# Fused state-space tables on VectorE, with the skip diagonal and the B clearing on ScalarE

## The chip, the core and the metric

The kernel runs on one core of a Trainium2 chip. The metric is the device time of one execution in microseconds. Three runs of the kernel before gave 884.39, 884.48 and 885.38 us, so the median is 884.48 us.

## The reference, cut to what matters

The program is a decoder trunk of two residual layers and a final RMSNorm, over 256 tokens of width 2048, in float32. Layer 0 projects the normalised input to 5120 columns (xa, ga, u, v, gb). The columns xa go through a complex-diagonal state-space mixer of 64 groups with 64 states each; u, v and gb go through a gated MLP. Layer 1 is differential attention. The change touches the constants of the state-space mixer and one small exponential of layer 1.

```python
dt = exp(log_dt)[:, None]
mag = exp(lr * dt)
ab_re = mag * cos(li * dt)
ab_im = mag * sin(li * dt)
...
bb_re = f_re[..., None] * br - f_im[..., None] * bi
...
# h: scan of the states with a = ab over the 256 positions
y = einsum(h_re, c_re) - einsum(h_im, c_im) + d_skip * u
```

## The kernel before

All weights stream once from HBM in chunks of 1 MB, in the order v, xa, u, gb, ga, then the output projection of layer 0 and the weights of the GLU, then layer 1. A chunk lands in one of three buffers `wr`. It is split into two halves, and each half into two parts so that TensorE can multiply float32 as products of a shorter format: ScalarE writes the rounded part `wh` (line 82, called from `split`, line 193), and VectorE writes the remainder `wl` (line 61, called from line 194). `wh` and `wl` have three buffers each, one per half, so the half number n can be written only when TensorE has finished with the half n - 3. The activations are split the same way into `hh` (ScalarE) and `hl` (VectorE), tile by tile, while the first four chunks are split (`h_split`, line 311). For each weight tile and each token half TensorE runs three matmuls, `wh` with `hh`, `wl` with `hh`, and `wh` with `hl`.

The accumulators of the projections (`main_t`, `main_c`) are tiles of the tag "m" with two buffers. v has two of them (v0, v1), and xa0, the first tile of xa, reuses the buffer of v0. So xa0 can start only when v0 has been read out. That is done by two Gelu activations into `vt` (lines 673 and 674), which need the row scale `rs0` of the RMSNorm of the input; a table load for Gelu stands ahead of them.

The state-space constants are made in the meantime. `ssm_params` (line 388) computes dt and mag with `exact_exp` (line 359), a polynomial exponential of some 20 VectorE operations of 128x32, then the phase with a sine and a cosine polynomial, and seven repeated squarings `pw` (line 461). `e_tables` (line 558) builds for each half a table `E` of the powers of the phase for 128 positions, by doubling: for k = 1 to 6 it multiplies the first 2^k columns by `pw[k]` in blocks of 8 pairs. `ssm_consts` (line 492) clears the tiles `bbr` on GpSimd and fills them later. `diag_skip` (line 481) builds 16 diagonal blocks `intra` from the identity and the skip weights `dq`, on GpSimd.

Nothing of the order is written by hand, except on SyncE's queue. A list scheduler with its own cost model decides in which order each engine's instructions stand; the splits, the Gelu of v and the norm are marked as urgent (`hp()`), the constants are not. Each engine then runs its list strictly in order, so an instruction that waits holds up all that stands behind it.

Of the kernel before, what the change touches and what calls it, by code (L numbers as in the profile page):

```python
# [10 lines left out]
F32 = mybir.dt.float32  # L11
F32R = mybir.dt.float32r
I32 = mybir.dt.int32
AF = mybir.ActivationFunctionType
ALU = mybir.AluOpType
# [14 lines left out]
def hybrid_trunk_kernel(ctx: ExitStack, tc: tile.TileContext, xT, xtok, w_in0, w_glu, w_out0,  # L30
# [20 lines left out]
    def t4(name, shape, dt=F32):  # L51
        return tmp.tile(shape, dt, name=name, tag="t4", bufs=3)
# [10 lines left out]
    def mul(o, a, b):  # L63
        tt(o, a, b, ALU.mult)

    def add(o, a, b):
        tt(o, a, b, ALU.add)
# [4 lines left out]
    def ts(o, a, s1, op0, s2=None, op1=None):  # L72
        if op1 is None:
            V.tensor_scalar(out=o, in0=a, scalar1=s1, scalar2=None, op0=op0)
        else:
            V.tensor_scalar(out=o, in0=a, scalar1=s1, scalar2=s2, op0=op0, op1=op1)
# [278 lines left out]
    def tr32(name, shape=(128, 32), dt=F32):  # L355
        return sm.tile(list(shape), dt, name=name, tag=f"tr{shape[1]}{'i' if dt == I32 else ''}",
                       bufs=(7 if dt == F32 else 1) if shape[1] <= 32 else 2)

    def exact_exp(o, x, w=32):
        sh = (128, w)  # L360
        xc = tr32("e_x", sh)
        ts(xc, x, -104.0, ALU.max, 90.0, ALU.min)
        n = tr32("e_n", sh)
        ts(n, xc, 1.4426950408889634, ALU.mult)
        ts(n, n, MAGIC, ALU.add)
        ts(n, n, MAGIC, ALU.subtract)
        r = tr32("e_r", sh)
        stt(r, n, -0.693359375, xc, ALU.mult, ALU.add)
        stt(r, n, 2.12194440054690583e-4, r, ALU.mult, ALU.add)
        p = tr32("e_p", sh)  # L370
        ts(p, r, 1.0 / 5040, ALU.mult)
        for c in (1.0 / 720, 1.0 / 120, 1.0 / 24, 1.0 / 6, 0.5, 1.0):
            stt(p, p, c, r, ALU.add, ALU.mult)
        ts(p, p, 1.0, ALU.add)
        n1 = tr32("e_n1", sh)
        ts(n1, n, 0.5, ALU.mult)
        ts(n1, n1, MAGIC, ALU.add)
        ts(n1, n1, MAGIC, ALU.subtract)
        sub(n, n, n1)
        for part in (n1, n):  # L380
            e = tr32("e_i", sh, I32)
            ts(e, part, 127.0, ALU.add, 8388608.0, ALU.mult)
            mul(p, p, e.bitcast(F32))
        V.tensor_copy(out=o, in_=p)

    cst = {}

    def ssm_params():
        dt_ = p32("dt")
        exact_exp(dt_, log_dt)  # L390
        yield
        mag = p32("mag")
        z = tr32("lrdt")
        mul(z, lam_re, dt_)
        exact_exp(mag, z)
        r2 = p32("r2")
        mul(r2, mag, mag)
        cst["r2"] = r2
        yield
        ph = tr32("ph")  # L400
        mul(ph, lam_im, dt_)
        k = tr32("ph_k")
        ts(k, ph, 1.0 / (2 * math.pi), ALU.mult)
        ts(k, k, MAGIC, ALU.add)
        ts(k, k, MAGIC, ALU.subtract)
        stt(ph, k, -6.28125, ph, ALU.mult, ALU.add)
        stt(ph, k, -1.93500518798828125e-3, ph, ALU.mult, ALU.add)
        stt(ph, k, -(2 * math.pi - 6.28125 - 1.93500518798828125e-3), ph, ALU.mult, ALU.add)
        y = tr32("ph_y")
        ts(y, ph, 0.5, ALU.mult)  # L410
        z = tr32("ph_z")
        mul(z, y, y)
        s = tr32("ph_s")
        f = math.factorial
        ts(s, z, 1.0 / f(13), ALU.mult)
        for c in (-1.0 / f(11), 1.0 / f(9), -1.0 / f(7), 1.0 / f(5), -1.0 / f(3)):
            stt(s, s, c, z, ALU.add, ALU.mult)
        stt(s, s, 1.0, y, ALU.add, ALU.mult)
        c_ = tr32("ph_c")
        ts(c_, z, -1.0 / f(14), ALU.mult)  # L420
        for c in (1.0 / f(12), -1.0 / f(10), 1.0 / f(8), -1.0 / f(6), 1.0 / f(4), -0.5):
            stt(c_, c_, c, z, ALU.add, ALU.mult)
        ts(c_, c_, 1.0, ALU.add)
        ep = p32("ep", 64).rearrange("p (c m) -> p c m", c=2)
        mul(ep[:, 0, :], s, s)
        ts(ep[:, 0, :], ep[:, 0, :], -2.0, ALU.mult, 1.0, ALU.add)
        stt(ep[:, 1, :], s, 2.0, c_, ALU.mult, ALU.mult)
        yield
        ab = p32("ab", 64).rearrange("p (c m) -> p c m", c=2)
        mul(ab, ep, mag.unsqueeze(1).to_broadcast([128, 2, 32]))  # L430
        den = tr32("den")
        t1 = tr32("t1")
        mul(den, lam_re, lam_re)
        mul(t1, lam_im, lam_im)
        add(den, den, t1)
        V.reciprocal(out=den, in_=den)
        nr = tr32("nr")
        ts(nr, ab[:, 0, :], 1.0, ALU.subtract)
        fc = p32("fc", 64).rearrange("p (c m) -> p c m", c=2)
        t2_ = tr32("t2")  # L440
        mul(t1, nr, lam_re)
        mul(t2_, ab[:, 1, :], lam_im)
        add(t1, t1, t2_)
        mul(fc[:, 0, :], t1, den)
        mul(t1, ab[:, 1, :], lam_re)
        mul(t2_, nr, lam_im)
        sub(t1, t1, t2_)
        mul(fc[:, 1, :], t1, den)
        fa = p32("fa", 64).rearrange("p (c m) -> p c m", c=2)
        mul(t1, fc[:, 0, :], ab[:, 0, :])  # L450
        mul(t2_, fc[:, 1, :], ab[:, 1, :])
        sub(fa[:, 0, :], t1, t2_)
        mul(t1, fc[:, 0, :], ab[:, 1, :])
        mul(t2_, fc[:, 1, :], ab[:, 0, :])
        add(fa[:, 1, :], t1, t2_)
        cst.update(ab=ab, fc=fc, fa=fa, ep=ep)
        yield

        pw = []
        prev = ep  # L460
        for j in range(7):
            sq = tr32("pw_sq", (128, 64)).rearrange("p (c m) -> p c m", c=2)
            m = tr32("pw_m")
            mul(sq, prev, prev)
            add(m, sq[:, 0, :], sq[:, 1, :])
            ts(m, m, -1.0, ALU.mult, 2.0, ALU.add)
            e = p32(f"pw{j}", 64).rearrange("p (c m) -> p c m", c=2)
            sub(e[:, 0, :], sq[:, 0, :], sq[:, 1, :])
            stt(e[:, 1, :], prev[:, 0, :], 2.0, prev[:, 1, :], ALU.mult, ALU.mult)
            mul(e, e, m.unsqueeze(1).to_broadcast([128, 2, 32]))  # L470
            pw.append(e)
            prev = e
        cst["pw"] = pw
        yield
# [3 lines left out]
    def sc16(ap):  # L478
        return ap.unsqueeze(2).to_broadcast([128, 32, 16])

    def diag_skip():
        intra = t8(11, "intra", [128, 16, 128])
        for i in range(16):
            G.tensor_scalar(out=intra[:, i, :], in0=ident, scalar1=dq[:, i:i + 1], scalar2=None, op0=ALU.mult)
        cst["intra"] = intra

    def masked(dst, src):
# [4 lines left out]
    def ssm_consts():  # L492
        for c in range(2):
            bbr[c] = t8(7 + c, f"bbr{c}", [128, 32, 2, 32])
            G.memset(bbr[c], 0.0)
        cA = t8(9, "cA", [128, 2, 32, 32])
        cN = t8(10, "cN", [128, 2, 32, 32])
        G.memset(cA, 0.0)
# [59 lines left out]
    def e_tables(half):  # L558
        E = big.tile([128, 2, 16, 128], F32, name=f"E{half}", tag="e")
        etab[half] = E  # L560
        hs = slice(half * 16, half * 16 + 16)
        pw = cst["pw"]
        V.memset(E[:, 0, :, 0:1], 1.0)
        V.memset(E[:, 1, :, 0:1], 0.0)
        V.tensor_copy(out=E[:, :, :, 1:2], in_=pw[0][:, :, hs].unsqueeze(3))
        for k in range(1, 7):
            n = 1 << k
            for q in range(2):
                ph = slice(q * 8, q * 8 + 8)
                es = E[:, :, ph, 0:n]  # L570
                sh = [128, 8, n]
                m = [t4(f"em{half}{k}{q}{i}", [128, 2, 8, 64])[:, :, :, 0:n] for i in range(2)]
                for i in range(2):
                    a = pw[k][:, i, half * 16 + q * 8:half * 16 + q * 8 + 8].unsqueeze(2).to_broadcast(sh)
                    for c in range(2):
                        mul(m[i][:, c], es[:, c], a)
                o = slice(n, 2 * n)
                sub(E[:, 0, ph, o], m[0][:, 0], m[1][:, 1])
                add(E[:, 1, ph, o], m[0][:, 1], m[1][:, 0])
            if k >= 4:  # L580
                yield
        yield
# [81 lines left out]
    for n in range(2):  # L664
        ps = main_t(f"v{n}")
        for k in range(4):
            gemm_t(ps, h_acts, range(k * 4, k * 4 + 4), k == 0, k == 3)
            if n == 0 and k == 2:
                diag_skip()
            run_side(2)  # L670
        with hp():
            for t in range(2):
                act(vt[:, t, n * 512:(n + 1) * 512], ps[:, t, :], AF.Gelu_apprx_tanh,
                    scale=rsx[0][:, t:t + 1], accum_out=vsum[:, t, n:n + 1])
# [488 lines left out]
```

## Time and profile before

| | |
|---|---|
| median of three runs | 884.48 us |
| the profiled execution, its own time | 885.88 us |
| its span | 884.2 us |
| TensorE matmul, busy | 867.1 us (98%) |
| VectorE, busy | 678.4 us (77%), 1248 instructions |
| ScalarE, busy | 457.5 us (52%), 637 instructions |
| GpSimd, busy | 36.5 us (4%), 54 instructions |
| TensorE clock granted over the span | 0.998 |

The profile is of one execution. A busy share is an average over stages that have different limits. Matmuls overlap their neighbours, so a matmul's own duration is longer than the step from one to the next, and the step is what counts for the pace. 1.7 us of the profiled execution's time lie outside its span.

### The profile page before, as it was taken

The numbers are of one execution on the slowest core, as the hardware profiler recorded it, in microseconds if no ns is written. First come the engines' busy times: TensorE is split into PE (matmuls) and PEld (weight loads), VectorE is DVE, ScalarE is ACT, GpSimd is POOL, SyncE is SP. The second block draws the span as 40 slices with busy tenths as digits, with TensorE's granted clock in tenths as the row PEclk, the third lists the DMA queues.
The fourth block names the chain that finished last, engine by engine and source line by source line (L and its number), as shares of the span: only waits on it lengthen the run. The fifth ranks groups of instructions, "written<-read, shape, count | busy, mean of one in ns | idle before, by whom it ended". The sixth has DMA issues, their size and how long they took to land.

```text
span 884.2 us, 13006 instructions
## 1 busy us (share of the span) xinstructions
PE 867.1 (98%) x5038; PEld 748.3 (85%) x5038; DVE 678.4 (77%) x1248; ACT 457.5 (52%) x637; POOL 36.5 (4%) x54
## 2 busy tenths in 40 slices
PE   9999999999999999999999999999999999999996
PEld 7799978788999789888788888888888888888885
DVE  8999869999988766577876688667867687665773
ACT  6664862455434655565445544455546544564551
POOL 7100000000000100000000000000000000000001
PEclk9999999999999999999999999999999999999999
DMA  8965452235524655555554555445554555555442
GB/s 289 406 236 193 144 191 95 97 103 184 191 99 145 254 178 184 190 191 171 169 203 153 181 191 191 184 153 184 183 192 154 190 182 189 189 194 199 157 178 95
DMA packets 55166, 160.18 MB, mean 181 GB/s; under 512 B 3392, under 2 KB 37440, under 8 KB 41024
## 3 DMA queue, kind: packets, MB, share of 16 engines
q1 hardware_dynamic: 54240, 155.68, 50.1%
q0 software_dynamic: 576, 3.15, 0.9%
q8 instruction: 39, 0.64, 0.3%
q10 hardware_dynamic: 288, 0.52, 0.2%
q14 instruction: 23, 0.19, 0.1%
HBM read 157.24 MB, written 2.10 MB: 180 GB/s over the span
## 4 chain that ended last, share of the span: by engine, by line
PE 87%; DVE 8%; ACT 2%; issue 1%; DMA 1%; DVEq 0%; ACTq 0%
PE k L251 7%; PE q L251 7%; PE v L225 4%; PE v L226 4%; PE v L224 4%; PE k L252 3%; PE q L252 3%; PE g L226 3%; PE g L225 3%; PE g L224 3%; PE od L225 2%; PE od L224 2%; PE od L226 2%; DVE wl L61 2%; PE ga L237 2%; PE ga L240 2%
## 5 line engine op out<-in xcount | busy, mean ns | idle before, releaser
L82 ACT ACTIVATE wh<-wr 128x1024 fp32r<-128x1024 f32 (+1 forms) x276 | 288.7, 1047 | 339.2 <-PE v L226 59.5
L61 DVE TENSOR_TENSOR wl<-wr,wh 128x1024 fp32r<-128x1024 f32 (+1 forms) x276 | 332.3, 1206 | 135.3 <-ACT wh L82 133.8
L251 PE MATMUL k<-h2p,wh 128*128 128x512 f32 x256 | 90.9, 398 | 1.7 <-DVE rm L61 1.7
L251 PE MATMUL q<-h2p,wh 128*128 128x512 f32 x256 | 90.2, 396 | 0.0
L252 PE MATMUL q<-h2p,wl 128*128 128x256 f32 x256 | 71.9, 284 | 0.2 <-DVE wl L61 0.2
L252 PE MATMUL k<-h2p,wl 128*128 128x256 f32 x256 | 72.0, 282 | 0.0
L251 PEld LDWEIGHTS k<-h2p,wh 128*128 128x128 f32 x256 | 48.1, 188 | 13.3 <-DVE rm L61 2.0
L251 PEld LDWEIGHTS q<-h2p,wh 128*128 128x128 f32 x256 | 47.8, 188 | 10.5
L225 PE MATMUL v<-wl,h2p 128*128 128x512 f32 x128 | 50.8, 397 | 0.0
L225 PE MATMUL g<-wl,h2p 128*128 128x512 f32 x128 | 50.3, 393 | 0.0
L226 PE MATMUL g<-wh,h2p 128*128 128x512 f32 x128 | 50.1, 391 | 0.0
L226 PE MATMUL v<-wh,h2p 128*128 128x512 f32 x128 | 50.0, 391 | 0.0
L224 PE MATMUL g<-wh,h2p 128*128 128x512 f32 x128 | 50.0, 390 | 0.0
L224 PE MATMUL v<-wh,h2p 128*128 128x512 f32 x128 | 50.0, 390 | 0.0
L252 PEld LDWEIGHTS q<-h2p,wl 128*128 128x128 f32 x256 | 48.4, 189 | 1.0 <-DVE wl L61 0.6
L252 PEld LDWEIGHTS k<-h2p,wl 128*128 128x128 f32 x256 | 48.4, 189 | 0.1
L225 PE MATMUL od<-wl,oh 128*128 128x512 f32 x96 | 37.6, 392 | 0.0
L224 PE MATMUL od<-wh,oh 128*128 128x512 f32 x96 | 37.5, 391 | 0.0
L226 PE MATMUL od<-wh,ol 128*128 128x512 f32 x96 | 37.3, 390 | 0.0
L237 PE MATMUL ga<-hh,wh 128*128 128x256 f32 x128 | 36.6, 286 | 0.0
L240 PE MATMUL ga<-hh,wl 128*128 128x256 f32 x128 | 36.5, 287 | 0.0
L239 PE MATMUL ga<-hl,wh 128*128 128x256 f32 x128 | 36.5, 285 | 0.0
(330 smaller groups left out, 2041.1 us busy)
## 6 DMA issues: line engine op xcount, KB each, us to landing
wr<-in_w_in_dram SPq DMA_DIRECT2D x68, 1024.0 KB, 4.8
wr<-in_w_in_dram SPq DMA_DIRECT2D x68, 512.0 KB, 5.2
wr<-in_w_out_dram SPq DMA_DIRECT2D x32, 1024.0 KB, 4.8
wr<-in_w_glu_dram SPq DMA_DIRECT2D x4, 1024.0 KB, 4.7
wr<-in_w_in_dram SPq DMA_DIRECT2D x8, 256.0 KB, 4.9
xk<-in_xtok_dram SPq DMA_DIRECT2D x2, 1024.0 KB, 10.8
xr<-in_xtok_dram POOLq DMA_DIRECT2D x2, 1024.0 KB, 7.2
xt<-in_xT_dram SPq DMA_DIRECT2D x8, 128.0 KB, 4.6
```

What stands on the lines that cost most here:

```text
L61: (eng or V).tensor_tensor(out=o, in0=a, in1=b, op=op)
L82: A.activation(out=o, in_=i, func=f, **kw)
L224: PE.matmul(ps[:, t, :], hi[:, s], wh, start=first and a == 0, stop=False)
L225: PE.matmul(ps[:, t, :], hi[:, s], wl, start=False, stop=False)
L226: PE.matmul(ps[:, t, :], lo[:, s], wh, start=False, stop=last and a == len(ktiles) - 1)
L237: PE.matmul(ps[:, c, :], wh[:, s], hi, start=first and a == 0 and c % 2 == 0, stop=False, skip_group_check=True)
L239: PE.matmul(ps[:, c, :], wh[:, s], lo, start=False, stop=False, skip_group_check=True)
L240: PE.matmul(ps[:, c, :], wl[:, s], hi, start=False, stop=fin, skip_group_check=True)
L251: PE.matmul(ps[:, c, :], wh[:, s], hl, start=first and a == 0, stop=False, skip_group_check=True)
L252: PE.matmul(ps[:, c, T:], wl[:, s], hl[:, 0], start=False, stop=a == len(ktiles) - 1 and not first, skip_group_check=True)
```

## The change

The exponential loses four VectorE operations each time: two scalings are fused with the addition behind them, the final addition of 1 goes into the first product, and the second product writes the result directly. The phase loses one operation, and each of the seven squarings loses one. The power tables multiply both parts (real and imaginary) in one operation, in blocks of up to 16 pairs: a half took 72 operations, and now takes 28. The clearing of `bbr` and the 16 diagonal blocks go from GpSimd to ScalarE, and the call of `diag_skip` stands three chunks later in the program.

```diff
@@ exact_exp
-        ts(n, xc, 1.4426950408889634, ALU.mult)
-        ts(n, n, MAGIC, ALU.add)
+        ts(n, xc, 1.4426950408889634, ALU.mult, MAGIC, ALU.add)
         ts(n, n, MAGIC, ALU.subtract)
...
-        ts(p, p, 1.0, ALU.add)
         n1 = tr32("e_n1", sh)
-        ts(n1, n, 0.5, ALU.mult)
-        ts(n1, n1, MAGIC, ALU.add)
+        ts(n1, n, 0.5, ALU.mult, MAGIC, ALU.add)
         ts(n1, n1, MAGIC, ALU.subtract)
         sub(n, n, n1)
-        for part in (n1, n):
-            e = tr32("e_i", sh, I32)
-            ts(e, part, 127.0, ALU.add, 8388608.0, ALU.mult)
-            mul(p, p, e.bitcast(F32))
-        V.tensor_copy(out=o, in_=p)
+        e = tr32("e_i", sh, I32)
+        ts(e, n1, 127.0, ALU.add, 8388608.0, ALU.mult)
+        stt(p, p, 1.0, e.bitcast(F32), ALU.add, ALU.mult)
+        e = tr32("e_i", sh, I32)
+        ts(e, n, 127.0, ALU.add, 8388608.0, ALU.mult)
+        mul(o, p, e.bitcast(F32))
@@ ssm_params
-        ts(k, ph, 1.0 / (2 * math.pi), ALU.mult)
-        ts(k, k, MAGIC, ALU.add)
+        ts(k, ph, 1.0 / (2 * math.pi), ALU.mult, MAGIC, ALU.add)
...
-            add(m, sq[:, 0, :], sq[:, 1, :])
-            ts(m, m, -1.0, ALU.mult, 2.0, ALU.add)
+            stt(m, sq[:, 0, :], -1.0, sq[:, 1, :], ALU.mult, ALU.subtract)
...
-            mul(e, e, m.unsqueeze(1).to_broadcast([128, 2, 32]))
+            stt(e, m.unsqueeze(1).to_broadcast([128, 2, 32]), 2.0, e, ALU.add, ALU.mult)
@@ diag_skip, ssm_consts
+    def zeros(z):
+        act(z.rearrange("p m j h -> p (m j h)").rearrange("p (a b) -> p a b", b=128),
+            ones.unsqueeze(1).to_broadcast([128, 16, 128]), AF.Copy, scale=0.0)
...
-            G.tensor_scalar(out=intra[:, i, :], in0=ident, scalar1=dq[:, i:i + 1], scalar2=None, op0=ALU.mult)
+            act(intra[:, i, :], ident, AF.Copy, scale=dq[:, i:i + 1])
...
-            G.memset(bbr[c], 0.0)
+            zeros(bbr[c])
@@ e_tables
-            for q in range(2):
-                ph = slice(q * 8, q * 8 + 8)
+            w = min(16, 512 // n)
+            for ph in (slice(z, z + w) for z in range(0, 16, w)):
...
-                    for c in range(2):
-                        mul(m[i][:, c], es[:, c], a)
+                    mul(m[i], es, a.unsqueeze(1).unsqueeze(3).to_broadcast([128, 2, w, n]))
@@ the loop over v
-            if n == 0 and k == 2:
+            if n == 1 and k == 0:
                 diag_skip()
```

The scheduler makes new lists from this. Three places of them follow, before and after; equal rows that stand together are counted (x2).

The first place is the head of ScalarE's list. `warm` is a one-column activation, `hh` a tile of the input's rounded part, and `wr_89` the first chunk. Before:

```order
L82 ACT_TABLE_LOAD
L82 ACTIVATE warm<-ones 128x1
L82 ACTIVATE hh_152<-xt,pkt 128x256
L82 ACTIVATE wh_0_156<-wr_89 128x512
L82 ACTIVATE hh_152<-xt,pkt 128x256
L82 ACTIVATE wh_0_156<-wr_89 128x512
```

And now:

```order
L82 ACT_TABLE_LOAD
L82 ACTIVATE warm<-ones 128x1
L82 ACTIVATE bbr_557<-ones 128x2048
L82 ACTIVATE bbr_559<-ones 128x2048
L82 ACTIVATE intra<-ident,pkt 128x128 x11
L82 ACTIVATE hh_152<-xt,pkt 128x256 x3
L82 ACTIVATE wh_0_156<-wr_89 128x512 x2
```

Both clearings, 11 of the 16 diagonal blocks and two further tiles of `hh` now stand ahead of the first `wh`.

The second place is VectorE's list about the first `wl`, in the projection of v. Before, seven instructions stand ahead of the first `hl`, and the first `wl` comes four small operations behind it:

```order
L79 SCALAR_TENSOR_TENSOR hl_154<-xt,pkt,hh_152 128x256
L79 SCALAR_TENSOR_TENSOR e_r<-e_n,e_r 128x32
L74 TENSOR_SCALAR e_p<-e_r 128x32
L74 TENSOR_SCALAR e_n_231<-e_n 128x32
L79 SCALAR_TENSOR_TENSOR e_p<-e_p,e_r 128x32
L61 TENSOR_TENSOR wl_0_157<-wr_89,wh_0_156 128x512
```

And now:

```order
L79 SCALAR_TENSOR_TENSOR hl_154<-xt,pkt,hh_152 128x256
L79 SCALAR_TENSOR_TENSOR ph<-ph_k,ph 128x32
L79 SCALAR_TENSOR_TENSOR e_p<-e_p,e_r 128x32
L79 SCALAR_TENSOR_TENSOR hl_154<-xt,pkt,hh_152 128x256
L79 SCALAR_TENSOR_TENSOR ph<-ph_k,ph 128x32
L79 SCALAR_TENSOR_TENSOR hl_154<-xt,pkt,hh_152 128x256
L79 SCALAR_TENSOR_TENSOR e_p<-e_p,e_r 128x32
L61 TENSOR_TENSOR wl_0_157<-wr_89,wh_0_156 128x512
```

Ahead of the first `hl` now stand 34 small operations of the two exponentials and the phase, and three `hl` stand ahead of the first `wl`.

The third place is ScalarE's list where v0 is read out. The name wh7_1 is the second half of chunk 7, the last chunk of v; chunk 8 is the first of xa. Before:

```order
L82 ACTIVATE wh7_0_860<-wr7_125 128x1024
L82 ACTIVATE wh7_1_864<-wr7_125 128x1024
L82 ACTIVATE cN_649<-bct_85 64x32x16 x4
L82 ACT_TABLE_LOAD
L82 ACTIVATE vt_210,vsum_211<-v0_402,rs0_186 128x512 x2
L82 ACTIVATE wh8_0_894<-wr8_128 128x1024
L82 ACTIVATE wh8_1_898<-wr8_128 128x1024
```

And now:

```order
L82 ACTIVATE wh7_1_794<-wr7_125 128x1024
L82 ACTIVATE wh8_0_824<-wr8_128 128x1024
L82 ACTIVATE wh8_1_828<-wr8_128 128x1024
L82 ACTIVATE wh9_0_961<-wr9_788 128x1024
L82 ACT_TABLE_LOAD
L82 ACTIVATE vt_210,vsum_211<-v0_386,rs0_186 128x512 x2
L82 ACTIVATE vt_210,vsum_211<-v1_639,rs0_186 128x512 x2
```

The table load and the read-out of v0 moved behind wh8_0, wh8_1 and wh9_0. The buffer of wh9_0 is that of wh7_1, three halves earlier.

## Rows read from the trace of the kernel before

**Rows 1.** The page: the chain that ended last, share of the span by engine.

```profile
PE 87%; DVE 8%; ACT 2%; issue 1%; DMA 1%; DVEq 0%; ACTq 0%
```

**Rows 2.** Busy time in stretches (start:end, length, then busy us by engine, clock, DMA).

```profile
5.50:54.20 48.70, 46.80 (x198) 37.59 (x197) 46.78 (x203) 34.21 (x50) 17.45 (x19) 1.00 0.95 362
54.20:103.70 49.50, 49.50 (x520) 49.11 (x520) 48.49 (x99) 27.00 (x36) 0.00 (x0) 1.00 0.48 171
103.70:288.90 185.20, 181.80 (x1227) 157.55 (x1226) 163.74 (x287) 87.12 (x105) 0.00 (x0) 1.00 0.40 140
```

**Rows 3.** Timeline of ScalarE, start of the program (start us, us, instruction, [idle before]).

```profile
2.10 0.20 ACT L82 ACTIVATE warm<-ones 128x1 f32<-128x1 f32 x1
3.58 0.51 ACT L82 ACTIVATE hh<-xt,pkt 128x256 fp32r<-128x256 f32 x1 [1.27 <-DMA xt<-in_xT_dram]
5.01 0.63 ACT L82 ACTIVATE wh<-wr 128x512 fp32r<-128x512 f32 x1 [0.92 <-DMA wr<-in_w_in_dram]
...
16.25 0.91 ACT L82 ACTIVATE hh<-xt,pkt 128x256 fp32r<-128x256 f32 x2
```

**Rows 4.** Timeline of TensorE, from the warm-up matmuls into v.

```profile
1.13 4.64 PE L298 MATMUL psw<-ones 128*128 128x128 f32 x20 [1.13 <-DVE ones L293]
5.69 0.79 PE L224 MATMUL v<-wh,hh 128*128 128x512 f32 x1
7.47 0.79 PE L225 MATMUL v<-wl,hh 128*128 128x512 f32 x1 [0.99 <-DVE wl L61]
8.06 0.63 PE L226 MATMUL v<-wh,hl 128*128 128x512 f32 x1
8.49 0.63 PE L224 MATMUL v<-wh,hh 128*128 128x512 f32 x1
...
10.58 0.40 PE L226 MATMUL v<-wh,hl 128*128 128x512 f32 x1
10.81 0.39 PE L224 MATMUL v<-wh,hh 128*128 128x512 f32 x1
```

**Rows 5.** Timelines of GpSimd and VectorE: clearings, and what VectorE ran then.

```profile
0.99 3.54 POOL L495 MEMSET bbr<- 128x2048 f32 x2
...
2.73 1.84 DVE L76 TENSOR_SCALAR e_x<-pkt 128x32 f32<-128x32 f32 x1 [1.65 <-DMA pkt<-in_pk_dram]
...
37.06 0.18 DVE L61 TENSOR_TENSOR pw_m<-pw_sq 128x32 f32<-128x32 f32 x1
...
37.23 1.81 POOL L499 MEMSET cN<- 128x2048 f32 x1 [1.03 <-ACT xsq L82]
...
37.36 1.22 DVE L61 TENSOR_TENSOR wl<-wr,wh 128x1024 fp32r<-128x1024 f32 x1
```

**Rows 6.** Timeline of VectorE in the second half's power table, and two plain splits.

```profile
218.55 2.49 DVE L61 TENSOR_TENSOR em<-E,pw 128x512 f32<-128x512 f32 x4
...
223.90 2.39 DVE L61 TENSOR_TENSOR wl<-wr,wh 128x1024 fp32r<-128x1024 f32 x2
```

**Rows 7.** Timeline of ScalarE at the read-out of v0.

```profile
49.12 1.28 ACT L82 ACT_TABLE_LOAD   x1
50.41 0.69 ACT L82 ACTIVATE vt<-v,rs 128x512 f32<-128x512 f32 x1
...
51.09 0.68 ACT L82 ACTIVATE vt<-v,rs 128x512 f32<-128x512 f32 x1
...
51.75 2.00 ACT L82 ACTIVATE wh<-wr 128x1024 fp32r<-128x1024 f32 x2
```

**Rows 8.** Timeline of TensorE, the last matmul of v and the first of xa.

```profile
53.94 0.48 PE L226 MATMUL v<-wh,hl 128*128 128x512 f32 x1
54.25 0.28 PE L237 MATMUL xa<-hh,wh 128*128 128x256 f32 x1
```

**Rows 9.** Timeline of TensorE: a wait within v, and the longest wait after the start.

```profile
43.02 0.50 PE L225 MATMUL v<-wl,hh 128*128 128x512 f32 x1 [0.86 <-DVE wl L61]
...
430.82 0.51 PE L251 MATMUL k<-h2p,wh 128*128 128x512 f32 x1 [1.72 <-DVE rm L61]
```

More of the change, by code (lines that the diff above doesn't have):

```diff
@@ L567, in e_tables @@
             n = 1 << k
-            for q in range(2):
-                ph = slice(q * 8, q * 8 + 8)
+            w = min(16, 512 // n)
+            for ph in (slice(z, z + w) for z in range(0, 16, w)):
                 es = E[:, :, ph, 0:n]
-                sh = [128, 8, n]
-                m = [t4(f"em{half}{k}{q}{i}", [128, 2, 8, 64])[:, :, :, 0:n] for i in range(2)]
+                m = [t4(f"em{half}{k}{ph.start}{i}", [128, 2, w, n]) for i in range(2)]
                 for i in range(2):
-                    a = pw[k][:, i, half * 16 + q * 8:half * 16 + q * 8 + 8].unsqueeze(2).to_broadcast(sh)
-                    for c in range(2):
-                        mul(m[i][:, c], es[:, c], a)
+                    a = pw[k][:, i, half * 16 + ph.start:half * 16 + ph.stop]
+                    mul(m[i], es, a.unsqueeze(1).unsqueeze(3).to_broadcast([128, 2, w, n]))
                 o = slice(n, 2 * n)
```

## The prediction

> **What bounds the kernel now.** I read the page first: the chain that ended last is 87% TensorE [rows 1], and TensorE is busy 98% of the span. So VectorE's saved operations are worth only what TensorE waits for, and a new wait of TensorE is paid in full. Next come the busy times by stretch [rows 2]. From 5.5 to 54.2 us (v) TensorE is idle 48.70 - 46.80 = 1.9 us, from 54.2 to 103.7 (xa) not at all, and from 103.7 to 288.9 (where the power tables are used) 185.20 - 181.80 = 3.4 us. VectorE is busy 46.78, 48.49 and 163.74 us there: near its limit in the first two, and yet TensorE lost nothing in the second. Then the timelines, at three places. At the start the first `wh` runs at 5.01 us for 0.63 [rows 3], and TensorE begins v at 5.69 and goes on at 7.47, after the first `wl` [rows 4]. At the end of v, ScalarE has read out v0 by 51.8 [rows 7], and xa follows v after 0.31 us (53.94 to 54.25) [rows 8]. Last, two waits of TensorE: 0.86 us on a `wl` within v, and 1.72 us at 430.82, the longest after the start [rows 9].
>
> **The change, part by part.** The profiled execution took 885.88 us, 1.7 beyond its span of 884.2, and lies 1.4 above the median; I sum changes of the span and add them to the median.
>
> *The start.* ScalarE now runs two clearings, 11 diagonal blocks and three `hh` ahead of the first `wh`. Two `wh` of 1024 columns take 2.00 us [rows 7], so 2048 columns in one instruction cost about 1.9. For a block: two `hh` of 256 columns take 0.91 [rows 3], some 0.42 from one to the next; the columns cost 2.00/2048 x 128 = 0.12 per 128, which leaves 0.31 for 128. From the warm-up's end at 2.2: 2 x 1.9 + 11 x 0.31 + 3 x 0.42 = 8.5, so the first `wh` starts at 10.7, ends at 11.3, and its `wl` (half of 1.22 [rows 5], and a little) is there at 12.0. TensorE goes on at 12.0 instead of 7.47: **+4.5 us**. If a block costs only what the one-column `warm` does (0.20 [rows 3]) it is 11 x 0.11 = 1.2 less, and if it costs as much as an `hh`, 1.2 more: +3.3 to +5.7. I take the middle because the columns' price is measured on the same engine.
>
> VectorE doesn't set this. Its chain starts with `pkt` at 2.73; 34 operations at 0.18 [rows 5] end at 8.8, before the third `hh`. A fused operation has no row of its own; at up to twice 0.18 the chain would end near 12 and shift the start by about 1 more, which the upper end nearly holds. The first `e_x`, 1.84 us while GpSimd cleared `bbr`, falls to the usual 0.18 [rows 5]: 1.7 us on VectorE, hidden behind ScalarE.
>
> [...]
>
> *GpSimd.* Its 3.54 us of clearings and the blocks behind them go [rows 5]. What follows in its queue is the clearing of `cA`, which waits for the norm anyway, so the empty queue is worth nothing by itself. The trace shows no harm of a GpSimd clearing to a large two-input operation: `wl` took 1.22 us at 37.36, wholly beside `cN` [rows 5], as two of them took 2.39 elsewhere [rows 6]. So I count no faster `hl` or `wl` for the blocks removed. [...]
>
> *SyncE's queue.* The load of the fourth chunk waits for a buffer that the first chunk's splits free, so it slips with the start. TensorE needs it later by as much: 0.
>
> *Within v.* VectorE has about 20 small operations less over the whole program, 0.1 to 0.18 each, thus 2 to 3.6 us, most of them ahead of the tables; and TensorE, coming later, leaves VectorE more time. I let the 0.86 us wait [rows 9] and a little more go: **-1.0** (0 to -1.9, all the idle time of this stretch [rows 2]).
>
> *The read-out of v0.* This is the new wait. `wh9_0` now stands ahead of the table load on ScalarE. Its buffer is that of `wh7_1`, which TensorE reads to the last matmul of v. Only after that come `wh9_0` (0.97), the table load (1.28), and two `vt` (0.69 and 0.68) [rows 7], and only then is the buffer free that xa0 needs. Counted from the start of v's last matmul, which lasts about 0.39 [rows 4]: 0.39 + 0.97 + 1.28 + 0.69 + 0.68 = 4.0, where xa now follows after 0.31 [rows 8]: **+3.7 us**. It is 2.7 if the buffer were free early. It is 4.4 if `rs0`, which the read-out needs too, comes later by four of VectorE's small operations (4 x 0.18). Behind the table load stand v1's read-out and the next `wh`, which xa needs later.
>
> *The tables.* A half takes 28 operations instead of 72, 88 fewer in all. Four of 512 columns took 2.49 us, two of 1024 take 2.39 [rows 6]: 0.05 per operation saved, and more for small ones (a 128x32 one is 0.18, nearly all of it fixed). At 0.06 it is 5.3 us. In the xa stretch TensorE was never idle, so that share is worth nothing; from 103.7 on 3.4 us could come back. Other engines' evacuations end part of these waits, so I take about half: **-1.6** (0 to -3.4).
>
> *Later.* The `lame` exponential saves four tiny operations; the 1.72 us wait at 430.82 [rows 9] is for `rm`, not for it: 0.
>
> Sum: 4.5 - 1.0 + 3.7 - 1.6 = **+5.6 us**, so 884.48 + 5.6 = **890.1 us**. By the bounds alone it lies between 3.3 - 1.9 + 2.7 - 3.4 = +0.7 and 5.7 + 4.4 = +10.1.
>
> **The rivals.**
>
> *The slow pace comes back before xa.* TensorE waits about 4 us at the end of v. If it then runs as at the start, six steps of 0.42 in place of 0.23 (8.06 to 10.58 [rows 4]) are lost, 1.2 us: 891.3. For it: the start did run so, although the warm-up matmuls had ended only at 5.77. Against it: after the wait of 1.72 us the matmul at 430.82 took 0.51 and the pace behind it was full, but that wait is shorter. [...]
>
> *No wait at the end of v.* If the read-out of v0 comes out early after all (the buffer of `wh9_0` free in time, the table load ahead of v's end), 3.7 goes: +1.9, 886.4. Against it: both engines follow their lists strictly, and the buffer is three halves old.
>
> *Faster.* If VectorE sets the pace between 54 and 289 us, its saving (5.3 for the tables, 2 for small ones, 1.7 for `e_x`, 9.0 in all) turns into time: 8.2 - 9.0 = -0.8, 883.7. It decides once more than 8.2 us come back. For it: VectorE is busy 48.49 of 49.50 us in the xa stretch [rows 2]. Against it: TensorE lost nothing there, and its idle time in v and the tables' stretch is 5.3 us in all [rows 2], less than the two losses.
>
> That the change doesn't do what it says is excluded: the lists of instructions show the moves.
>
> **How the numbers follow.** The forecast has 0.62, the slow pace 0.18, no wait at the end of v 0.08, faster 0.06; the last 0.06 is for sums beyond these. The range runs from 886.8, just above the rival without the wait, to 893.6: the sum with the start and the read-out at their upper ends (+1.2 and +0.7) and the slow pace (1.2) is 893.2, and some 0.4 less given back. About 0.2% (1.8 us) is what a measurement can tell from no change: slower is above 886.25. Faster 0.06, the same 0.08 (the rival at 886.4 lies on this edge), slower 0.86.
>
> **What the changed profile would show.** If right: ScalarE's `bbr` and `intra` from 2.2 us to 9.4, the first `wh` near 10.7, TensorE's second matmul of v near 12.0; at the end of v a wait of xa of 3.5 to 4 us that is ended by ScalarE's `vt`, with `wh9_0` and the table load right ahead of it; TensorE's idle time in the tables' stretch near 1.8 us instead of 3.4; `e_x` at 0.18. It would be wrong if the first `wh` ran before 8 us, if xa followed v without a wait, or if TensorE's idle time after xa fell by more than the two waits add, or grew.

## The result and the profile after

Four runs of the changed kernel gave 892.63 to 893.60 us, median 893.12; the kernel before, on the same chip, 884.93 (four runs). The ratio is 1.0088, with a 95% interval of 1.0076 to 1.0100: slower by 8.2 us. The forecast was 890.1, and its range (886.8 to 893.6) holds the time near its upper end. The profiled execution has a span of 891.9 us instead of 884.2, so 7.7 us are to be found.

The head of ScalarE, in its timeline (start us, us, instruction, [idle before]), to be set beside [rows 3]:

```profile
2.21 3.70 ACT L82 ACTIVATE bbr<-ones 128x2048 f32<-128x2048 f32 x2
5.82 3.30 ACT L82 ACTIVATE intra<-ident,pkt 128x128 f32<-128x128 f32 x11
9.03 1.29 ACT L82 ACTIVATE hh<-xt,pkt 128x256 fp32r<-128x256 f32 x3
10.22 1.65 ACT L82 ACTIVATE wh<-wr 128x512 fp32r<-128x512 f32 x3
```

The clearings take 1.85 us each, the blocks 0.30 (3.30 / 11), and the first `wh` runs at 10.22 where it ran at 5.01. TensorE's timeline shows what that does, beside [rows 4]:

```profile
10.89 0.79 PE L224 MATMUL v<-wh,hh 128*128 128x512 f32 x1 [5.12 <-ACT wh L82]
11.89 0.79 PE L225 MATMUL v<-wl,hh 128*128 128x512 f32 x1 [0.21 <-DVE wl L61]
12.48 0.63 PE L226 MATMUL v<-wh,hl 128*128 128x512 f32 x1
12.91 0.63 PE L224 MATMUL v<-wh,hh 128*128 128x512 f32 x1
...
16.16 0.39 PE L226 MATMUL v<-wh,hl 128*128 128x512 f32 x1
```

The second matmul comes at 11.89 instead of 7.47. The slow pace (0.43 us from one to the next) lasts 8 steps instead of 6.

The read-out of v0 in ScalarE's timeline, beside [rows 7]:

```profile
59.55 1.06 ACT L82 ACTIVATE wh<-wr 128x1024 fp32r<-128x1024 f32 x1 [2.41 <-PE v L226]
60.62 1.28 ACT L82 ACT_TABLE_LOAD   x1
61.92 0.69 ACT L82 ACTIVATE vt<-v,rs 128x512 f32<-128x512 f32 x1
...
62.60 0.68 ACT L82 ACTIVATE vt<-v,rs 128x512 f32<-128x512 f32 x1
```

and TensorE's from the last matmul of v on, beside [rows 8]:

```profile
59.13 0.39 PE L226 MATMUL v<-wh,hl 128*128 128x512 f32 x1
63.42 0.39 PE L237 MATMUL xa<-hh,wh 128*128 128x256 f32 x1 [3.91 <-ACT vt L82]
...
64.21 0.41 PE L239 MATMUL xa<-hl,wh 128*128 128x256 f32 x1
64.42 0.41 PE L240 MATMUL xa<-hh,wl 128*128 128x256 f32 x1
...
67.29 0.28 PE L239 MATMUL xa<-hl,wh 128*128 128x256 f32 x1
67.41 0.28 PE L240 MATMUL xa<-hh,wl 128*128 128x256 f32 x1
```

`wh9_0` waits 2.41 us for the end of v, and the chain behind it is the one that was forecast. xa follows v's last matmul after 4.29 us (0.31 before). Then its matmuls come 0.21 us apart, and only from 67.2 on 0.12. The busy times in stretches (start:end, length, then busy us by engine, granted clock, DMA) show the granted clock fall and come back:

```profile
64.00:68.00 4.00, 4.00 (x23) 4.00 (x23) 3.73 (x8) 0.70 (x3) 0.00 (x0) 0.61 0.59 242
68.00:72.00 4.00, 4.00 (x36) 4.00 (x35) 2.88 (x4) 2.17 (x3) 0.00 (x0) 1.00 0.20 37
```

The 0.61 is a mean over a stretch in which the clock changed: it reads 0.50 from 64 to 67 us and 1.00 from 67.3 to 68.

Last, what TensorE waited for in the whole program (line, what it waited for, us in total, times, longest):

```profile
PE v L224 <- ACT wh L82: 5.1, 1, 5.1
PE xa L237 <- ACT vt L82: 3.9, 1, 3.9
...
PE v L225 <- DVE wl L61: 1.6, 3, 0.9
PE u L225 <- DVE wl L61: 1.4, 1, 1.4
...
PE xa L240 <- DVE wl L61: 0.7, 1, 0.7
```

The first two are the forecast's two losses. The same view of the kernel before had 1.9 us on `wl` in v, 1.4 on `ut` at the start of gb, 0.8 on `bT` and 0.8 on a `wl` of u.

The 7.7 us of span, taken at the same four points of both timelines:

| stretch | before | after | difference | forecast |
|---|---|---|---|---|
| to the second matmul of v | 7.47 | 11.89 | +4.4 | +4.5 |
| from there to the last matmul of v | 46.47 | 47.24 | +0.8 | -1.0 |
| from there to the first of xa | 0.31 | 4.29 | +4.0 | +3.7 |
| slow pace at the head of xa | 0 | 1.6 | +1.6 | 0 (a rival: +1.2) |
| the rest, to the end | 829.95 | 826.9 | -3.1 | -1.6 |

The slow pace is worked out from the rows: from 63.42 to 67.29 there are 19 steps, which at 0.12 us take 2.3 us instead of 3.9. VectorE's busy time fell from 678.4 to 668.7 us, 9.7 us (9.0 forecast), with 1140 instructions instead of 1248.

### The profile page after: what moved, and what is told of

Its sections match the earlier page's. It is cut to its first block, busy times and chain, and to the rows that moved or that the text cites. A ratio compares the mean times of both kernels' runs of the same rounds, so it can differ in the third digit from the quotient of the medians.

```text
span 891.9 us, 12898 instructions
## 1 busy us (share of the span) xinstructions
PE 867.7 (97%) x5038; PEld 749.5 (84%) x5038; DVE 668.7 (75%) x1140; ACT 467.1 (52%) x656; POOL 21.7 (2%) x36
## 4 chain that ended last, share of the span: by engine, by line
PE 85%; DVE 8%; issue 2%; DMA 2%; ACT 1%; SPq 0%; DVEq 0%; ACTq 0%
PE k L251 7%; PE q L251 7%; PE v L225 3%; PE k L252 3%; PE v L226 3%; PE v L224 3%; PE q L252 3%; PE g L226 3%; PE g L225 3%; PE g L224 3%; PE od L225 2%; PE od L224 2%; PE od L226 2%; DVE wl L61 2%; PE ga L240 2%
## 5 line engine op out<-in xcount | busy, mean ns | idle before, releaser
L237 PE MATMUL xa<-hh,wh 128*128 128x256 f32 x128 | 37.1, 290 | 3.9 <-ACT vt L82 3.9
L240 PE MATMUL xa<-hh,wl 128*128 128x256 f32 x128 | 37.3, 291 | 0.7 <-DVE wl L61 0.7
L239 PE MATMUL xa<-hl,wh 128*128 128x256 f32 x128 | 37.1, 290 | 0.0
```

The lines of the kernel that those rows point to most:

```text
L237: PE.matmul(ps[:, c, :], wh[:, s], hi, start=first and a == 0 and c % 2 == 0, stop=False, skip_group_check=True)
L239: PE.matmul(ps[:, c, :], wh[:, s], lo, start=False, stop=False, skip_group_check=True)
L240: PE.matmul(ps[:, c, :], wl[:, s], hi, start=False, stop=fin, skip_group_check=True)
```

## Experiments

Twelve kernels were run, in four groups, each beside the kernel before on the same chip. Differences are against that kernel's median (885.5 to 886.0 us in these groups).

**The two halves alone.** `fuse_only` keeps the VectorE part and leaves both ScalarE moves out:

```diff
-            zeros(bbr[c])
+            G.memset(bbr[c], 0.0)
-            act(intra[:, i, :], ident, AF.Copy, scale=dq[:, i:i + 1])
+            G.tensor_scalar(out=intra[:, i, :], in0=ident, scalar1=dq[:, i:i + 1], scalar2=None, op0=ALU.mult)
-            if n == 1 and k == 0:
+            if n == 0 and k == 2:
```

> The VectorE half of the change alone: fused exponentials, phase and tables; the B tiles and the diagonal stay on GpSimd, called where they were. In ScalarE's list the first wh is back at its old place, and the table load and the read-out of v0 stand ahead of wh9_0. Theory (the loss is made by ScalarE's new work at the start and by the read-out that stands behind wh9_0, not by the fused operations): TensorE's second matmul of v near 7.5 to 8.6 us, no wait of over 1 us before xa, matmuls of xa 0.12 us apart from the first, 885 us (883.5 to 887). Rival (the fused, wider operations hold up the splits): waits of TensorE on wl add up to several us in v and xa, 889 or more.

Measured: 889.89 against 885.97, ratio 1.0049 (1.0032 to 1.0066), 3.9 us slower. Both theories missed. The marks of the first came as expected (second matmul at 7.43, xa 0.12 us apart). The rival's time came, but not its mechanism: the waits on `wl` in v and xa rose from 1.9 to 3.5 us, yet xa started only 0.1 us later than before. The loss stands further back, in TensorE's waits:

```profile
PE gb L224 <- ACT ut L82: 2.3, 1, 2.3
PE s L723 <- DVE ut L79: 1.9, 1, 1.9
```

and in its timeline at the second of them:

```profile
136.83 0.39 PE L226 MATMUL u<-wh,hl 128*128 128x512 f32 x1
139.16 1.16 PE L723 MATMUL s<-vt,bw 128*128 128x128 f32 x8 [1.94 <-DVE ut L79]
...
141.12 0.63 PE L224 MATMUL u<-wh,hh 128*128 128x512 f32 x1
141.54 0.63 PE L225 MATMUL u<-wl,hh 128*128 128x512 f32 x1
```

In this list the product `s` of the second round stands right behind the last matmul of a tile of u. It needs what ScalarE reads out of that tile (`ut`) and VectorE then works on, so it can't be ready. Before, other products stand between the two, and `s` did not wait. Behind this wait the slow pace comes back: until 144 us the matmuls of u are 0.43 us apart, not 0.23 (granted clock 0.57 from 140 to 144). The wait for `s` (1.9), the slow steps (some 1.4) and the longer wait of gb (2.3 instead of 1.4) come to 4.2 us; from xa on this run lost 4.4, so the rest nearly cancels.

`move_only` is the other half: clearing and diagonal by ScalarE in the kernel before, VectorE untouched.

> The ScalarE half alone: clearings and diagonal blocks by ScalarE, all VectorE operations as before the change. The first wh is late as in the changed kernel, but the table load and the read-out of v0 stand ahead of wh7_1. Theory: second matmul of v near 12 us (+4.5 to +4.7), no wait of over 1.5 us before xa, 887.5 us (886 to 890). Rival (the wait before xa comes with the late start, whatever the order): a wait of 3 to 4 us before xa and the slow pace behind it, 892 to 894.

Measured: 887.67, 1.0023 (1.0012 to 1.0034), 1.7 us slower, as the theory had it. The second matmul comes at 12.04, and no wait of TensorE before xa is over 0.5 us, since in this list the table load stands ahead of `wh7_1`. So the late start alone doesn't make the wait before xa. Neither half has that wait; only both together do. The halves' losses don't add up either: 3.9 + 1.7 is 5.6, and the change lost 8.2.

**The start alone mended.** `late_dep` holds the clearings and blocks back until the last `hh`:

```diff
-            ones.unsqueeze(1).to_broadcast([128, 16, 128]), AF.Copy, scale=0.0)
+            hh[1][:, 7, 0:128].bitcast(F32).unsqueeze(1).to_broadcast([128, 16, 128]), AF.Copy, scale=0.0)
...
+        dl = p32("dl", 16)
+        stt(dl, hh[1][:, 7, 0:16].bitcast(F32), 0.0, dq, ALU.mult, ALU.add)
```

> The whole change, but ScalarE's clearings and diagonal blocks can't start before the last hh: the clearings read a tile of hh (times zero) instead of the ones, and the diagonal's scales are copied behind it by one more VectorE operation. wh9_0 still stands ahead of the table load. Theory (two separate losses): the start is back at 7.0 to 7.5 us, the wait of about 4 us before xa and the slow pace behind it stay, 888.5 us (887 to 890). Rival (the wait before xa is a consequence of the late start): it goes too, 884 to 885.5.

Measured: 894.10, 1.0099 (1.0084 to 1.0114), 8.1 us slower: not faster than the change itself. The start was mended more than expected (second matmul at 6.39, full pace from there), and the wait of 3.9 us before xa and the slow pace stayed, so these two are separate losses. The forecast of 888.5 missed all the same, because the work that left the start is in the way later. From ScalarE's timeline:

```profile
24.26 3.72 ACT L82 ACTIVATE bbr<-hh 128x2048 f32<-128x2048 f32 x2
27.89 1.04 ACT L82 ACTIVATE wh<-wr 128x1024 fp32r<-128x1024 f32 x1
28.83 3.31 ACT L82 ACTIVATE intra<-ident,dl 128x128 f32<-128x128 f32 x11
```

TensorE waits 4.2 us on `wl` and 1.4 on `wh` within v in this run, and 1.9 for the early `s`; the slow pace at the head of xa is longer, too (until 67.1).

**What the slow pace is.** `fill` adds 16 products between v and xa in the changed kernel:

```diff
+    with tc.issue_after(last_mm[0]):
+        for _ in range(16):
+            PE.matmul(psx, hh[0][:, 0, 0:128], fill, start=True, stop=True)
```

> The changed kernel with 16 added products of 512 columns, whose result nobody reads, queued on TensorE right behind the last matmul of v, so that it isn't idle while it waits for the read-out of v0; the read-out is held behind wh9_0 as in the changed kernel. Theory (the slow pace of the first xa matmuls, 0.21 us instead of 0.12, comes from the idle 3.9 us ahead of them): xa starts as long after v as before, within 0.3 us, its matmuls are 0.12 us apart from the first, and 1.6 us go: 891.5. Rival (something else slows them, for instance their operands): they stay at 0.21, 893.1.

Measured: 890.89, 1.0061 (1.0046 to 1.0076), 4.9 us above before, thus 3.3 less than the change. TensorE's timeline:

```profile
58.37 0.39 PE L234 MATMUL v<-wh,hl 128*128 128x512 f32 x1
58.60 3.79 PE L711 MATMUL psx<-wh,hh 128*128 128x512 f32 x16
62.67 0.39 PE L245 MATMUL xa<-hh,wh 128*128 128x256 f32 x1 [0.28 <-ACT vt L679]
62.89 0.28 PE L247 MATMUL xa<-hl,wh 128*128 128x256 f32 x1
63.01 0.28 PE L248 MATMUL xa<-hh,wl 128*128 128x256 f32 x1
```

xa starts 4.30 us after the last matmul of v, as without the fill (4.29), and its matmuls are 0.12 us apart behind the first (granted clock 1.00 from 60 to 68 us). The pace is thus set by TensorE's idleness, not by xa's operands. That accounts for 1.6 us; the rest of the gain is not the pace: the new list also lost 1.0 us of the waits on `wl` in v (0.6 instead of 1.6) and the 0.7 us on a `wl` in xa.

**The wait before xa alone, mended and made.** `gelu_first` is the change with `wh9_0` queued behind the read-out:

```diff
+                        if (i, b) == (9, 0):
+                            with tc.issue_after(v_read[0]):
+                                act(h[:, e], w[:, e], AF.Copy)
```

> The changed kernel with one edge more: on ScalarE, wh9_0 is queued behind the table load and the read-out of v0 instead of ahead of them. All else is the whole change, the late start too. Theory (the wait before xa is made by wh9_0's place alone, and the slow pace by the wait): second matmul of v still near 12 us; wait before xa 1 to 1.5 us (the table load and two read-outs still stand behind wh8_1), its matmuls 0.12 us apart; 888.5 us, 4.5 less than the changed kernel (3.5 to 5.5 less). Rival (the read-out is late because the row scale rs0 comes late from VectorE): a wait of 3 us or more stays, 892 to 893.

Measured: 890.25, 1.0052 (1.0037 to 1.0067), 4.7 us above before and 3.5 less than the change. The wait before xa is 2.16 us, with full pace behind it. It is longer than expected, and the reason is the one the rival named, in a smaller size. ScalarE's timeline:

```profile
57.23 1.28 ACT L677 ACT_TABLE_LOAD   x1
60.21 0.69 ACT L677 ACTIVATE vt<-v,rs 128x512 f32<-128x512 f32 x1 [1.70 <-DVE rs L79]
```

The table is loaded at 58.5, but `rs0` comes at 60.1. In the changed kernel it was just as late, and stood hidden behind `wh9_0`:

```profile
55.44 2.35 DVE L61 TENSOR_TENSOR wl<-wr,wh 128x1024 fp32r<-128x1024 f32 x2
57.71 2.35 DVE L61 TENSOR_TENSOR em<-E,pw 128x1024 f32<-128x1024 f32 x2
59.98 0.15 DVE L79 SCALAR_TENSOR_TENSOR rs<-rq_z,rs 128x2 f32<-128x2 f32 x1
```

The last step of the norm, 0.15 us of work, stands behind two splits and two of the new wide table operations.

`wait_only` puts nothing but that order into the kernel before, the read-out held behind `wh9_0`:

```diff
+                        if (i, b) == (9, 0):
+                            for z in v_read:
+                                tc.add_manual_dep(z, r.ins.name, mybir.DependencyInfo(
+                                    mybir.DependencyClass.NoSync, mybir.DependencyReason.DATA), reason="order")
```

> The kernel before with nothing of the change in it but its order at one place: on ScalarE the table load and the read-out of v0 and v1 are held behind wh9_0. Theory: the start as before (second matmul at 7.5 us), a wait of 4 us before xa, matmuls of xa 0.21 us apart for some 3.5 us behind it, and a few tenths at the first splits of xa; 5 us more than before (4 to 6 more). Rival (what is lost there is made good by the stages behind, where VectorE and ScalarE get ahead): 1 to 3 us more than before.

Measured: 889.07, 1.0046 (1.0031 to 1.0061), 3.5 us slower by the medians and 4.1 by the ratio: at the lower edge of the theory. The wait before xa is 3.9 us, the matmuls behind it are 0.21 apart until 61.2 (1.6 us lost), and `wl` in xa costs 1.4 us. Part of this is made good, as the rival had it: the profiled span is only 2.8 us longer (887.0). Its v ran without slow steps at the start and took 0.9 us less, and what comes behind the slow pace took 2.0 us less than before, with the 1.4 us on `wl` in it; gb, for one, waits 0.4 us instead of 1.4.

**The VectorE half in two.** `small_only` has the fused exponential, phase and squarings (20 operations fewer), `tables_only` the wide tables (88 fewer); all else is as before.

> Only the fused exponential, phase and squarings (20 small VectorE operations fewer); power tables, clearings and diagonal as before. Theory (the fused operations are cheaper, and the 4 us that the VectorE half lost came from the places of the products s and gb in TensorE's list, which wait for ut): without those places nothing is lost, the 0.9 us wait within v and the 1.5 us wait of gb shrink, 1 to 3.5 us less than before. Rival (the fused small operations put more of them ahead of the splits and cost time): 2 us more or worse.

> Only the power tables in 28 wider operations a half instead of 72; exponential, phase, squarings, clearings and diagonal as before. Theory (as for small_only: a list without the two late places of s and gb): between 1.5 less and 1 more than before, with a new wait of TensorE of 1 to 1.5 us on a wl in xa, since one table operation of 1024 columns now stands ahead of a split. Rival (wider table operations are what made the VectorE half slow): 3 us more or worse, with the waits of s and gb for ut in it.

Measured: `small_only` 884.38, 0.9988 (0.9979 to 0.9998), 1.2 us faster; `tables_only` 886.48, 1.0009 (1.0000 to 1.0018), 0.9 us slower, with a wait of 1.8 us on a `wl` in xa. Both times lie where the theory had them: neither part alone has the late `s`, and neither costs more than 1 us. Of the marks, gb's wait of 1.4 us is gone in `small_only`, but the waits on `wl` in v grew from 1.9 to 3.1 us instead of shrinking. Together the two parts are `fuse_only`, 3.9 us slower with VectorE less busy (671.5 us) than in either (676.9 and 672.1). The changed kernel has the same VectorE operations as `fuse_only`, and behind the slow pace it is 3.1 us faster than before. So the 3.9 us are no cost of the fused operations themselves; they come with places in a list. That the two places named above are all of it is argued from the waits: no run puts them back in `fuse_only`.

**Toward a better version.** All the operations of the change with both places mended is `late_queue`: the clearings and blocks queued behind the last `hh`, after which the scheduler itself puts the read-out of v0 ahead of `wh8_1` and `wh9_0`.

```diff
+            with tc.issue_after(last_hh[0]):
+                zeros(bbr[c])
...
+                with tc.issue_after(last_hh[0]):
+                    diag_skip()
```

> The whole change, with ScalarE's clearings and diagonal blocks queued behind its last hh; the list that results has the table load and the read-out of v0 ahead of wh8_1 and wh9_0. So both places at which the changed kernel lost time are mended and all its operations are kept. Theory (the clearings and blocks cost ScalarE 8 us that it doesn't have while it splits the chunks of v): second matmul of v near 6.4 us, no wait over 1.5 us before xa, but waits of 3 us or more on wh and wl within v; 1 to 4 us more than before. Rival (with both places mended the saved VectorE time shows): 1 us less than before, or better.

Measured: 892.71, 1.0080 (1.0066 to 1.0094), 6.9 us slower. The place is as the theory said, the price is higher: two clearings and 11 blocks stand together ahead of the splits of v1, and TensorE waits for them once for nearly 4 us. The slow pace follows (steps of 0.43 us, granted clock 0.50 from 32 to 36 us), and comes once more behind the 1.54 us wait before xa (0.63 from 60 to 64 us).

```profile
24.07 3.71 ACT L82 ACTIVATE bbr<-ones 128x2048 f32<-128x2048 f32 x2
27.68 3.30 ACT L82 ACTIVATE intra<-ident,pkt 128x128 f32<-128x128 f32 x11
```

```profile
31.98 0.79 PE L224 MATMUL v<-wh,hh 128*128 128x512 f32 x1 [3.94 <-ACT wh L82]
```

What the start of the kernel before would gain if `e_x` weren't held [rows 5] was tried in two ways. First by shorter clearings, `before_pieces`, and with the fused small operations, `small_pieces`:

```diff
-            G.memset(bbr[c], 0.0)
+            for z in range(8):
+                G.memset(bbr[c][:, 4 * z:4 * z + 4], 0.0)
```

> The kernel before, with GpSimd clearing each bbr tile in 8 pieces of 256 columns instead of one of 2048. Theory (VectorE's first e_x was held for 1.66 us by one long clearing, and the first wl and TensorE's second matmul with it): e_x takes about 0.2 us or a few tenths, second matmul of v near 6.4 us instead of 7.4, 1 to 3 us less than before. Rival (the start is bound by the loads of the input and the weights, not by VectorE): second matmul of v at 7.4, no difference over 0.3 us.

> Two parts together: the fused exponential, phase and squarings of the change, and GpSimd clearing bbr in 8 pieces of 256 columns each; power tables in 72 operations a half and the diagonal on GpSimd, as before. Theory (both gains are waits of TensorE at different places, so they add): 2 to 5 us less than before. Rival (the earlier start is given back at the next transfer or split that is late): no more than small_only alone, 1 us less.

Measured: 886.47, 1.0012 (1.0003 to 1.0021), and 885.63, 1.0002 (0.9993 to 1.0010). The theory missed both times, and in `before_pieces` the rival too: the second matmul comes at 8.83 us, neither at 6.4 nor at 7.4. In `small_pieces` (8.76) the rival's outcome came: no more than `small_only` alone. GpSimd's and VectorE's timelines of `before_pieces`:

```profile
1.83 3.60 POOL L496 MEMSET bbr<- 128x256 f32 x14
```

```profile
2.89 2.57 DVE L76 TENSOR_SCALAR e_x<-pkt 128x32 f32<-128x32 f32 x1 [1.81 <-DMA pkt<-in_pk_dram]
```

`e_x` is held until 5.46, when the last of the pieces is done (5.43); it isn't let in between two of them.

The second way is `small_late`: the fused small operations, and only the two clearings on ScalarE, queued behind the splits; diagonal and tables as before.

```diff
-            G.memset(bbr[c], 0.0)
+            with tc.issue_after(last_wh[0]):
+                zeros(bbr[c])
```

> The fused exponential, phase and squarings as in small_only; the two clearings of bbr move from GpSimd to ScalarE, but queued behind the last hh, ahead of wh4_0; the diagonal stays on GpSimd and the power tables keep 72 operations a half. Theory (the hold of e_x ends with GpSimd's clearings, and ScalarE has the room there, since wh4_0 is needed only at 30 us): e_x under 0.9 us, second matmul of v at 6.8 us or earlier, no wait of over 1 us on wh within v, 1.5 to 5.5 us less than before. Rival (ScalarE's 3.7 us of clearings delay the splits of v as in late_queue): a wait of 2 us or more on a wh of v, no better than small_only (1 us less) or worse than before.

Measured: 883.86 against 885.53, 0.9981 (0.9972 to 0.9990), 1.7 us faster than before, where the change is 8.2 slower. `e_x` takes 0.18 us, the second matmul comes at 6.30, and full pace is reached at 7.2:

```profile
6.30 0.80 PE L227 MATMUL v<-wl,hh 128*128 128x512 f32 x1
...
7.21 0.40 PE L226 MATMUL v<-wh,hh 128*128 128x512 f32 x1
```

ScalarE's clearings at 24.35 to 28.06 cost TensorE nothing there; the longest wait within v is 0.8 us, on a `wl`. Of all versions it beats the kernel before most clearly. Its interval overlaps that of `small_only`, measured in another group, so what the earlier start is worth by itself is not shown.

## Why the prediction was right, and where it wasn't

*What bounds the kernel.* Right: TensorE. VectorE lost 9.7 us of work, and the time rose.

*The start.* Right in mechanism and size: +4.4 for +4.5. The block took 0.30 us (0.31 forecast), the clearing 1.85 (1.9), and VectorE's small operations ended at 8.6, ahead of the first `hh`'s arrival, so ScalarE set it. Two small misses cancel in it: the first `wh` came at 10.22 instead of 10.7, and its `wl` began at 11.15, some 0.3 us after that `wh`'s end, because it stood behind the third `hl` on VectorE. `move_only` shows the late start alone, `late_dep` the change without it.

*GpSimd.* A `wl` of 512 columns took 0.68 us with the blocks on GpSimd and without them, and the clearing of `cA` behind them waited for the norm as forecast.

*The read-out of v0.* Right: +4.0 for +3.7, by the very chain of the sum, with `wh9_0` at 1.06 us instead of 0.97 and small gaps between the links. `wait_only` makes it in the kernel before, and `gelu_first` takes it away. The condition for the upper end, a late `rs0`, was there as well, hidden behind `wh9_0`.

*The slow pace.* Here the forecast took the wrong case. It gave 0.18 to the rival that the pace comes back before xa, and argued against it from the wait of 1.72 us at 430.82 [rows 9], while saying that this wait was shorter. The rival came true, at 1.6 us (1.2 worked out). `fill` shows the cause: the same 4.3 us without idleness, and full pace. Where TensorE waited 3.9 us the granted clock behind it was low: 0.61 from 64 to 68 us in the changed kernel, 0.56 from 60 to 64 in `late_dep`. A shorter wait proves little either way: after 2.16 us in `gelu_first` the pace had not dropped (granted clock 1.00 from 60 to 64 us), after 1.94 us in `fuse_only` it had (0.57), and after 1.94 us ahead of the same product in `late_dep` it had not (1.00 from 154 to 158 us).

*Within v.* Wrong in sign: "I let the 0.86 us wait and a little more go: -1.0" became +0.8. About 0.4 of it are two more steps at the slow pace at the start (8 instead of 6, at 0.2 us). The rest are waits on `wl`, 1.4 us in two places late in v, that took the old one's place. The step that failed is the assumption that fewer operations leave VectorE more time there. With fewer small ones ahead, the scheduler moved more of the power tables up into v, in pieces of up to 1.2 us; in the kernel before, v holds only pieces of up to 64 columns. The first of the two `wl` stands behind such pieces. GpSimd's, VectorE's and TensorE's timelines:

```profile
49.44 2.36 DVE L61 TENSOR_TENSOR em<-E,pw 128x1024 f32<-128x1024 f32 x2
...
51.98 1.22 DVE L61 TENSOR_TENSOR wl<-wr,wh 128x1024 fp32r<-128x1024 f32 x1
52.37 3.13 POOL L657 TENSOR_SCALAR_AFFINE_SELECT bw<-bw 128x1024 f32<-128x1024 f32 x1 [10.12 <-DMA bw<-in_wsp_dram]
...
54.46 1.06 DVE L61 TENSOR_TENSOR rq_z<-rq_z,rq_v 128x2 f32<-128x2 f32 x1
```

```profile
53.26 0.50 PE L225 MATMUL v<-wl,hh 128*128 128x512 f32 x1 [0.93 <-DVE wl L61]
```

The second `wl`, at 55.44, for which TensorE waits 0.44 us, stands behind `rq_z`, a step of the norm on two columns. It took 1.06 us where 0.16 is usual, and ended when GpSimd's selection of `bw` ended (both at 55.5). So not all of the 1.4 us is the tables'.

*The tables.* Right in sign, mis-sized: -3.1 for -1.6 (bounds 0 to -3.4). The part that the forecast spoke of, TensorE's idle time, came out: from the first matmul of xa to the first of layer 1's q it was 349.45 - 345.68 = 3.8 us before and 347.93 - 345.74 = 2.2 after. In stretches, before and after:

```profile
54.25:403.70 349.45, 345.68 (x2370) 305.07 (x2368) 289.13 (x476) 180.75 (x234) 3.71 (x8) 1.00 0.46 164
```

```profile
63.42:411.35 347.93, 345.74 (x2372) 306.89 (x2373) 272.39 (x382) 181.81 (x234) 3.68 (x8) 1.00 0.47 164
```

The other 1.5 us lie in stretches that the view counts as busy, and their cause stays open. And the reason given, VectorE's saved time, is not what decides. `fuse_only` saves about as much and loses 4.4 us in that very stretch; `small_only` saves 1.5 us of VectorE and gains 1.2. What these stretches cost depends on which product stands where in TensorE's list. That the changed kernel's list happens to be a good one there was luck.

So the sum of 5.6 was 2.1 short of the span's 7.7: 1.6 for the pace, 1.8 for v and 0.3 for the read-out, less 1.5 that the tables gave back more and 0.1 at the start. The medians differ by 0.5 more than the two spans, and the kernel before took 0.45 more in this comparison than the 884.48 that the forecast started from; with these, 890.1 becomes 893.1. That the time still lies within the range is in part luck: the misses in v and in the tables, +1.8 and -1.5, nearly cancel.

## What to carry to other kernels

Where one engine is busy 98% of the time, a saving on another is worth no more than the first one's waits; read what a change costs from the places to which it moves instructions, and ask of each moved one what it waits for and who is queued behind it. A wait of TensorE can cost more than its length: behind 3.9 us of it the slow pace took another 1.6. A scheduler with its own cost model makes a new list for every edit, and two harmless edits can make a bad list together: pin down the two or three places that matter (first split, read-out before a buffer is needed) by explicit order before judging an edit. Work given to an engine that is idle on average still needs a moment when nobody waits behind it: the same two clearings cost 4.4 us with the blocks at the start, nearly 4 with the blocks in the middle of v, and nothing alone in the middle of v.

## What the runs showed that was not expected

Clearings of 256 columns, 14 of them in a row, held VectorE's single-input `e_x` as the long ones do in the kernel before (1.84 us [rows 5]): 2.57 us, to the end of the last (`before_pieces`); with no clearing on GpSimd it takes 0.18 (`small_late`). A two-input `wl` beside a clearing was not held (1.22 us [rows 5]). What makes the difference between the two no row shows. Why `e_x` isn't let in between two clearings, no run tells. Nor does one tell why, beside the selection of `bw`, the two-column `rq_z` was held to its end (1.06 us) while the `wl` at 51.98 was not (1.22 us, as elsewhere).

The slow pace at the start varies where the gap does not. With the second matmul at 7.42 to 7.47 us, the kernel before and `fuse_only` ran 6 slow steps, while `small_only`, `tables_only` and `wait_only` ran none. With it at 6.17 to 6.39 (`late_dep`, `late_queue`, `small_late`) no run of steps of 0.43 us came, and with it at 8.8 us or later 6 to 13 of them. These are single profiled executions, so some 1.2 us of difference between two kernels can be this alone; what decides it within one gap stays open, as it does for the two waits of 1.94 us in `fuse_only` and `late_dep`.
